# Two more conv channel tiles in the in-projection's second part

## The chip, the cores and the metric

One core of one Trainium2 chip runs the whole kernel, in one launch. The metric is the device time of an execution in microseconds (us); smaller is better. Engines are named as in the profile: PE (TensorE), DVE (VectorE), ACT (ScalarE), POOL (GpSimd) and SP (SyncE, which here only issues DMAs).

## The reference

One layer of a decoder trunk over 1024 positions of 1024 channels, all float32:

```
h = rms_norm(x, g_mix)
z = h @ w_in + b_in                      # 1024 -> 7168
va, ga, xb, gb, sa, sb = split(z, [1024, 1024, 1536, 1536, 1024, 1024])

u = va * sigmoid(ga)
u = causal_depthwise_conv(u, width 31)
y_a = silu(layer_norm(u)) @ w_a_out

v = causal_depthwise_conv(xb, width 4)
r = sigmoid(v @ w_a + b_a), i = sigmoid(v @ w_x + b_x)     # 16 heads of 96, block-diagonal
a = exp(-8 r softplus(-lam));  v = scan(h = a h + sqrt(1 - a^2) i v)
y_b = (v * gelu(gb)) @ w_b_out

x = x + (sigmoid(sa) * y_a + sigmoid(sb) * y_b) @ w_o
x = x + square(relu(rms_norm(x, g_mlp) @ w_1)) @ w_2
out = rms_norm(x, g_final)
```

## The kernel before

Channels lie on the 128 partitions, positions along the free axis. z has 56 tiles of 128 channels: 8 of va, 8 of ga, 12 of xb, 12 of gb, 8 of sa, 8 of sb. Each float32 operand of a product is split in a high and a low part, and a product is three matmul passes (high x high, low x high, high x low). Weights are split by `split_dma`: ACT writes the negative weight into the low tile (L65), a POOL DMA adds the weight to it (L66), ACT writes the high tile (L67).

**First part of the in-projection** (43 to 361 us). Tiles are computed one by one, in the order of the list `CH`. A tile is 48 matmuls (`chunk_mm`, L726): 8 blocks of input channels x 3 passes x 2 halves of the positions. The loop over s takes one tile of `CH` a turn; such a turn is called a slot here. Slot s also evacuates tile s-1 on ACT and DVE:

- an xb tile becomes v by the conv of width 4 (`xb_out`: xb L474, v L477 on ACT, the rest on DVE, L486), and `xb_parts` splits v (vth on ACT L494, vtl on DVE);
- a pair of va and ga becomes u = va x sigmoid(ga) (`u_out`, sigmoid L589 on ACT, the rest on DVE).

The 16 heads of the recurrence run in the same slots. Slot s of head n (`HS0[n]` = s): three quarters of the tile's matmuls, then the gate product of the head before (`head_mm(before, 1)`), the rest of the tile, then `head_mm(n, 0)`, the first gate product of the new head. Each is 6 matmuls (L534 to L536) on pieces of v (`head_load`, tiles vh and vl, loaded by SP at the end of the slot before). ACT reads the product with a sigmoid (`head_gate`, L542), and SP moves the gate to full tiles (L549). PSUM holds four tiles of 128 x 1024: three under the tag "ps" for the channel tiles, and one under "ps2" for all gate products (`PS`, L48). Heads stand in `HS0` in groups of four with one slot between (5-8, 10-13, 15-18, 20-23); a group's heads use three tiles of v. In the slot behind a group's last head (`EXP`: 9, 14, 19, 24) ACT computes the group's exponentials and tanh (`scan_exp`, L558, L559), in the next its square roots (`scan_root`, L566); then DVE runs the scans (`scan_tile`, L575 to L578, hd written by SP at L579). Exponentials, square roots and sigmoids each need their table loaded on ACT (ACT_TABLE_LOAD rows). The order of ACT's work in a slot is the order of these lines (shortened):

```
before, new, nxt = (head_at.get(s + d) for d in (-1, 0, 1))
if before is not None:
    head_gate(before, 0, begun)
    head_mm(before, 1)
...                                  # evacuation of tile s-1, weights of tile s+1
if s - 1 in EXP:
    scan_root(EXP[s - 1])
if s == 3 or c >= XB:
    vector_work(0)
    xb_parts(0 if s == 3 else c - XB)
if before is not None:
    head_gate(before, 1, clk["P"] - 12 * MM)
...                                  # then scan_exp in the slots of EXP
```

**Second part** (361 to 630 us). The other tiles are taken in pairs (`ZPAIRS`, 14 of them: gb, sa, sb), each as a 2 x 2 block product by Strassen's scheme with seven products of 12 matmuls (`z_mm`, L914) instead of eight. Its right sides are sums of quarters of the normalized input: `x_load` loads four xs tiles, `x_sum` forms the differences on DVE, `x_parts` splits them (xs6h, xs6l and so on); `XS` and `ZX` say in which slot. Its left sides are sums of quarters of the weights (`z_sums`, zs on DVE), split by `z_lhs` (zo). `z_out` evacuates a quarter: gb is multiplied with the scan's output, sa and sb are spilled as sigmoids.

**The conv of width 31** runs on DVE alone: for each of the eight u tiles some 48 operations (`conv`, taps L637), with a sum over tiles (ysum L651) for the layer norm's mean. A planner keeps a clock for PE, ACT and DVE (`clk`, `at`); `later` notes DVE work with a due time, `vector_work` issues it and fills what is left with taps. Order on each engine is fixed when the program is built.

**After it**: the product with w_b_out (8 tiles of 72 matmuls, `b_mm`, L1097), in which the conv's output is loaded again (`n_load`) and its mean formed (`n_mean`); then w_a_out, w_o and the MLP.

Of the kernel before, what the change touches and what calls it, by code (L numbers as in the profile page):

```python
# [15 lines left out]
P = 128  # L16
# [3 lines left out]
NH = 16  # L20
# [10 lines left out]
def trunk_kernel(ctx: ExitStack, tc: tile.TileContext, x, xt_in, xt_eo, vecs, w_in, w_a_out, w_b_out,  # L31
# [550 lines left out]
    yd = dp.tile([8, P, S], F32, name="yd")  # L582
    ysum = []

    def u_out(j, psv, psg):

        u = T(f"u{j}")
        uv = u.rearrange("p (o n) -> p o n", o=2)
        nc.scalar.activation(uv, psg.rearrange("p (n o) -> p o n", o=2), AF.Sigmoid,  # L589
                             bias=bin_c[:, GA + j:GA + j + 1])  # L590
        later(at("A", 1.11), 1.28, nc.vector.scalar_tensor_tensor, uv,
              psv.rearrange("p (n o) -> p o n", o=2), bin_c[:, VA + j:VA + j + 1], uv,
              ALU.add, ALU.mult)
        ut[j] = u
        fresh.append(j)


# [86 lines left out]
                later(at("A", 1.0), 1.2, nc.vector.tensor_tensor, l, src, h.bitcast(F32),  # L684
                      ALU.subtract)

    CH = [XB, VA, GA, XB + 1, XB + 2]
    for js, g in (((1,), 1), ((2,), 2), ((3,), 3), ((4, 5, 6, 7), 4)):
        CH += [c for j in js for c in (VA + j, GA + j)]
        CH += [XB + t for t in range(3 * g, min(3 * g + 3, 12))]  # L690
    NC1 = len(CH)
    zps = {n: z0[n] for n in range(N0)}
    wraw, wst = {}, {}
# [33 lines left out]
                                 start=n == 0, stop=n == 23)  # L727
        at("P", len(halves) * (n1 - n0) * MM)

    ZPAIRS = [GB + 2 * i for i in range(6)] + [SA + 2 * i for i in range(4)]  # L730
    ZPAIRS += [SB + 2 * i for i in range(4)]
    NZ = len(ZPAIRS)
    zraw, zs, zo, zb = {}, {}, {}, {}
# [2 lines left out]
    def z_load(i, kk):  # L736

        zraw[i, kk] = raw = qp.tile([P, 2, 4, P], F32, tag="p", name=f"zw{i}_{kk}", bufs=4)
        c = ZPAIRS[i]
        nc.sync.dma_start(raw, w_in[c:c + 2, :, 4 * kk:4 * kk + 4, :].rearrange("m p k c -> p m k c"))  # L740

    def z_blk(i, m_, kk):
# [45 lines left out]
    def z_get(n, f):  # L788
# [1 line left out]

    ENGINES = {mybir.EngineType.Activation, mybir.EngineType.DVE, mybir.EngineType.PE,
               mybir.EngineType.SP, mybir.EngineType.Pool}
    HS0 = [5 + 5 * (n // 4) + n % 4 for n in range(NH)]
    head_at = {s: n for n, s in enumerate(HS0)}

    EXP = {head_slot: g for g, head_slot in enumerate(HS0[4 * g + 3] + 1 for g in range(4))}
    XS = {23: ((x_load, 0),), 24: ((x_sum, 0),), 25: ((x_load, 1), (x_parts, 0, 6)),
          26: ((x_sum, 1), (x_parts, 0, 7, 5)), 27: ((x_parts, 0, 4), (x_parts, 1, 6))}
    w_load(3)
    w_load(4)  # L800
    for c2 in range(4):
# [2 lines left out]
    with tc.manual_schedule(engines=ENGINES):  # L804
        for s in range(3, NC1):
            w_load(s + 2)
            taps["hold"] = s > NC1 - 4
            begun = clk["P"]
            clk["A"], clk["V"] = max(clk["A"], begun + 0.5), max(clk["V"], begun - 2)

            if s == 3:

                chunk_mm(s, 0, 24, (1,))
                rs = first_scale()
                first_product(0, rs)
# [10 lines left out]
            if s > 3:  # L826
                chunk_mm(s, 18, 24)
            if new is not None:
                head_mm(new, 0)

            c = CH[s - 1]
            if c >= XB:
                xb_out(c - XB, zps[s - 1])
            elif c >= GA:
                u_out(c - GA, zps[s - 2], zps[s - 1])
            w_parts(s + 1)
            if s - 1 in EXP:

# [6 lines that stand above are left out]
            if nxt is not None:  # L845
                head_w_parts(nxt)
            if s == 5:
                decay_on()
            if s + 2 in head_at:
                head_w(head_at[s + 2])  # L850
            for d in range(5):
                if s - d in EXP:
                    g = EXP[s - d]
                    if d == 0:
                        scan_exp(g)
                        scan_in(begun + 3.5, 3 * g, 3 * g + 1)
# [49 lines left out]
    def z_mm(i, p):  # L906
# [9 lines left out]
                n += 1  # L916
        at("P", 12 * MM)

    def z_out(i, m_, hf, src, name):
        ci = ZPAIRS[i] + m_  # L920
        bias = bin_c[:, ci:ci + 1]
        if ci < SA:
# [19 lines left out]

    def z_h(i, m_, hf):
        t = ZPAIRS[i] + m_ - GB
        if t < 12:
            hb[t, hf] = h = EV(f"hb{t}_{hf}")
            nc.sync.dma_start(h, hd[t, :, HALVES[hf]])

# [26 lines left out]
        elif p == 4:  # L975
            z_out(i, 1, 0, zb[i, "u"], "c")

    ZX = {0: ((x_parts, 1, 7),), 7: ((later, 0, 4.8, scan_tile, 11),), 2: ((x_parts, 1, 5),), 4: ((x_parts, 1, 4),)}
    H_AT = {2: (0, 0), 5: (1, 1), 3: (0, 1), 4: (1, 0)}
    with tc.manual_schedule(engines=ENGINES):  # L980

# [36 lines left out]
        vector_work(clk["V"])  # L1018
        z_get(2, z_lhs)
        z_get(3, z_lhs)  # L1020
        u_out(7, zps[NC1 - 2], zps[NC1 - 1])
        vector_work(clk["V"])
        z_h(0, 0, 0)
        for n in range(len(zseq) + 2):
# [61 lines left out]
    def b_mm(j):  # L1086
# [11 lines left out]
        at("P", 72 * MM)  # L1098

    def b_out(j):  # L1100
        ps = bps.pop(j)
# [7 lines left out]

    q, mean, vacc, rstd = {}, {}, {}, {}  # L1110

    def n_load():
        for o in range(2):
            for kk in range(2):
                for c2 in range(2):
                    q[kk, o, c2] = a = T(f"q{kk}{o}{c2}")
                    for i in range(2):
                        nc.sync.dma_start(a[:, HALVES[i]], yd[4 * kk + 2 * c2 + i, :, HALVES[o]])

    def n_pieces(o):  # L1120
        return [(kk, c2, i) for kk in range(2) for c2 in range(2) for i in range(2)]
# [977 lines left out]
```

## Time and profile before

| | before |
|---|---|
| runs, us | 1545.78, 1543.67, 1544.39 (median 1544.39) |
| profiled execution, span, us | 1542.9 |
| PE busy | 1533.1 us (99%), 6782 instructions |
| DVE busy | 1222.5 us (79%) |
| ACT busy | 903.6 us (59%) |
| POOL busy | 184.4 us (12%) |
| granted TensorE clock, mean | 0.999 |
| first part, second part, product with w_b_out, us from the start | 43 to 361, 361 to 623, 623 to 760 |

The span runs from the first to the last instruction of one execution; the page gives no total of its own for that execution, and the median of the three runs stands 1.5 us above the span. A row of a timeline or of the chain has start, length (us), engine, line and operation, "out<-in" by the program's names, the count, and in brackets the engine's idle time ahead of it and what released it. Rows of stretches have start:end, length, then busy time and count for PE, PEld (weight load), DVE, ACT, POOL, and the granted clock, the share of the DMA engines and GB/s.

### The profile page before, as it was taken

The page shows a single profiled execution, that of the slowest core. Times are in us where ns is not written, and L with a number is a line of the kernel's source. Part 1 is how long each engine was busy: PE and PEld are TensorE (multiplying, and loading weights), DVE is VectorE, ACT ScalarE, POOL GpSimd, SP SyncE. Part 2 cuts the span into 40 slices and gives each one's busy share as a digit, 9 for nine tenths or more (in the row PEclk, how much of TensorE's full clock was granted, in tenths as well). Part 3 has the DMA queues.
Part 4 walks back from the last instruction along what each step waited for, and adds up shares of the span by engine and source line. Part 5 has one row for each costly group of instructions (what it writes and reads, how often), then busy time and mean ns, then how long its engine had stood idle before and what let it go on. Part 6 is the DMA issues. An engine that isn't in the chain of part 4 may idle for free.

```text
span 1542.9 us, 19178 instructions
## 1 busy us (share of the span) xinstructions
PE 1533.1 (99%) x6782; PEld 1262.4 (82%) x6782; DVE 1222.5 (79%) x1648; ACT 903.6 (59%) x1261; POOL 184.4 (12%) x219
## 2 busy tenths in 40 slices
PE   9999999999999999999999999999999999999998
PEld 8888788888888888888888887888888888888886
DVE  6899999979899997478569879755555558888897
ACT  6648576567567667345275777554444475555553
POOL 0000000002222222000022332000000001111110
PEclk9999999999999999999999999999999999999999
DMA  8776978898997879953579898333333779888862
GB/s 347 197 189 161 251 187 222 217 280 217 247 253 196 193 191 246 327 157 116 182 201 299 197 193 204 137 122 112 113 114 111 241 216 228 223 222 224 209 130 110
DMA packets 132288, 307.82 MB, mean 200 GB/s; under 512 B 13232, under 2 KB 35248, under 8 KB 132192
## 3 DMA queue, kind: packets, MB, share of 16 engines
q1 hardware_dynamic: 101744, 230.60, 46.0%
q0 software_dynamic: 30304, 75.74, 26.9%
q8 instruction: 53, 0.87, 0.2%
q14 instruction: 43, 0.35, 0.1%
q10 hardware_dynamic: 144, 0.26, 0.0%
HBM read 147.69 MB, written 58.72 MB: 134 GB/s over the span
## 4 chain that ended last, share of the span: by engine, by line
PE 95%; DMA 2%; issue 1%; DVE 1%; SPq 0%; POOL 0%; ACT 0%; POOLq 0%; DVEq 0%
PE z L726 18%; PE d L1863 15%; PE yb L1097 8%; PE e L1983 3%; PE keep L1863 2%; PE z L258 1%; PE rg L534 1%; PE rg L536 1%; PE rg L535 1%; DMA x<-in_x_dram 1%; DMA gu<-w_raw 1%; DMA xc<-in_xt_dram 0%; PE go3f L1274 0%; PE f15d L1550 0%; PE f15c L1550 0%
## 5 line engine op out<-in xcount | busy, mean ns | idle before, releaser
L726 PE MATMUL z<-xh,win_h 128*128 128x512 f32 x400 | 124.9, 390 | 0.0
L726 PE MATMUL z<-xl,win_h 128*128 128x512 f32 x400 | 124.5, 389 | 0.0
L1875 DVE TENSOR_TENSOR acc<-acc,d 128x1024 f32<-128x1024 f32 x72 | 87.8, 1219 | 33.3 <-PE d L1863 32.6
L726 PE MATMUL z<-xh,win_l 128*128 128x512 f32 x400 | 98.2, 391 | 0.0
L726 PEld LDWEIGHTS z<-xh,win_l 128*128 128x128 f32 x400 | 75.1, 188 | 16.9
L726 PEld LDWEIGHTS z<-xh,win_h 128*128 128x128 f32 x400 | 75.0, 188 | 16.7 <-ACT win_h L67 0.7
L637 DVE SCALAR_TENSOR_TENSOR y<-u,vec,y 128x511 f32<-128x511 f32 (+14 forms) x120 | 88.3, 736 | 0.0
L726 PEld LDWEIGHTS z<-xl,win_h 128*128 128x128 f32 x400 | 75.1, 188 | 15.8
L542 ACT ACTIVATE g<-rg,vec 96x1024 f32<-96x1024 f32 x32 | 35.6, 1113 | 85.5 <-issue 46.0
L637 DVE SCALAR_TENSOR_TENSOR y<-yt,csum,y 128x511 f32<-128x511 f32 (+6 forms) x112 | 82.5, 736 | 0.0
L637 DVE SCALAR_TENSOR_TENSOR yt<-u,vec,yt 128x511 f32<-128x511 f32 (+6 forms) x112 | 82.5, 736 | 0.0
L66 POOL DMA_DIRECT2D win_l<-win_raw x25 | 21.8, 871 | 324.3 <-ACT win_l L65 312.3
L1538 ACT ACTIVATE o<-s 128x512 fp32r<-128x512 f32 x56 | 33.7, 623 | 45.7 <-DVE s L1522 26.4
L66 POOL DMA_DIRECT2D zo<-zw x42 | 36.6, 871 | 129.4 <-ACT zo L65 116.1
L1097 PE MATMUL yb<-hgl,wb_h 128*128 128x512 f32 x168 | 51.7, 389 | 0.0
L1097 PE MATMUL yb<-hgh,wb_h 128*128 128x512 f32 x168 | 51.7, 389 | 0.0
L486 DVE SCALAR_TENSOR_TENSOR v<-xb,vec,v 128x1023 f32<-128x1023 f32 (+2 forms) x36 | 46.2, 1282 | 6.9 <-ACT v L477 6.1
L66 POOL DMA_DIRECT2D db_1l<-wr x7 | 6.1, 870 | 310.5 <-ACT db_1l L65 287.9
L1097 PE MATMUL yb<-hgh,wb_l 128*128 128x512 f32 x168 | 41.0, 389 | 0.0
L65 ACT ACTIVATE zo<-zw 128x512 fp32r<-128x512 f32 x42 | 26.3, 625 | 20.7 <-PE z10f L914 2.1
L1063 DVE TENSOR_TENSOR o<-s,o 128x512 fp32r<-128x512 f32 x56 | 37.3, 683 | 0.5 <-ACT o L1538 0.5
L1097 PEld LDWEIGHTS yb<-hgh,wb_h 128*128 128x128 f32 x168 | 31.5, 188 | 6.6
(1805 smaller groups left out, 4669.7 us busy)
## 6 DMA issues: line engine op xcount, KB each, us to landing
w_raw<-in_w_dram SPq DMA_DIRECT2D x34, 512.0 KB, 5.7
fr<-fd SPq DMA_DIRECT2D x32, 512.0 KB, 6.3
wr<-in_w_dram SPq DMA_DIRECT2D x32, 512.0 KB, 6.6
zw<-in_w_in_dram SPq DMA_DIRECT2D x28, 512.0 KB, 6.3
win_raw<-in_w_in_dram SPq DMA_DIRECT2D x25, 512.0 KB, 6.8
win_l<-win_raw POOLq DMA_DIRECT2D x25, 512.0 KB, 6.7
zo<-zw POOLq DMA_DIRECT2D x42, 256.0 KB, 5.6
gates<-zg SPq DMA_DIRECT2D x32, 256.0 KB, 3.9
```

Of the source, the lines that this page charges most:

```text
L65: nc.scalar.activation(l, src, AF.Copy, scale=-1.0)
L66: nc.gpsimd.dma_start(l, src, accum_op=ALU.add)
L486: nc.vector.scalar_tensor_tensor(v[:, d:S], a[:, 0:S - d], cbw_c[:, w * 12 + t:w * 12 + t + 1], v[:, d:S], ALU.mult, ALU.add)
L542: nc.scalar.activation(a, gps.pop((n, gi))[:HD, :], AF.Sigmoid, bias=(ba_c, bx_c)[gi][:, n:n + 1])
L637: nc.vector.scalar_tensor_tensor(o[:, k:], a[:, 0:HS - k], c, o[:, k:], ALU.mult, add)
L726: nc.tensor.matmul(zps[s][:, HALVES[hf]], w[:, k, :], xw[k][part][hf], start=n == 0, stop=n == 23)
L1063: tt(l, src, h.bitcast(F32), ALU.subtract)
L1097: nc.tensor.matmul(ps[hf], a, b[:, HALVES[hf]], start=n == 0, stop=n == len(todo) - 1)
L1538: nc.scalar.activation(o[:, 0], src, AF.Copy)
L1863: nc.tensor.matmul(o, a, b, start=n == 0 and (p != 1 or g == 0), stop=n == len(todo) - 1, skip_group_check=p == 1 and g > 0)
L1875: tt(acc[p, q2], acc[p, q2], ps, ALU.add)
L1983: nc.tensor.matmul(o, a, b, start=n == 0 and t not in LOADED, stop=n == len(todo) - 1, skip_group_check=t in LOADED)
```

## The change

- `NU = 6`: `CH` has va and ga of six conv tiles instead of eight, 24 tiles at its end instead of 28 (the first three are computed ahead of the loop). Its order becomes XB, VA, GA, XB1, XB2, GA1, XB3, VA1, XB4, XB5, GA2, XB6 to XB8, VA2, XB9 to XB11, then GA and VA of 3, 4, 5. ga now comes ahead of va, so `u_out` is cut in `u_gate` (the sigmoid) and `u_out` (the product), each with its own tile.
- `HS0` becomes 4 to 8 and 10 to 20: one slot without a new head (9) instead of three between the groups. `EXP` follows: 8, 13, 17, 21. Head 8 starts in 13, head 12 in 17.
- `ZPAIRS` gets the pairs (VA+6, GA+6) and (VA+7, GA+7) at places 6 and 8, 16 pairs in all. Their weights are loaded by two DMAs for each half; `z_out` hands them to the new `z_u`, which forms u6 and u7 by halves.
- `x_load`, `x_sum` and `x_parts` move to the last four slots; three of the x parts, (0,4), (1,6) and (1,7), go to the second part's first and second product.
- Of all groups the scans follow their roots by the same offset; `n_load` goes from j = 0 to j = 1 of the product with w_b_out, `n_mean` into the middle of tile 2.

```diff
-    CH = [XB, VA, GA, XB + 1, XB + 2]
-    for js, g in (((1,), 1), ((2,), 2), ((3,), 3), ((4, 5, 6, 7), 4)):
-        CH += [c for j in js for c in (VA + j, GA + j)]
-        CH += [XB + t for t in range(3 * g, min(3 * g + 3, 12))]
+    NU = 6
+    CH = [XB, VA, GA, XB + 1, XB + 2, GA + 1, XB + 3, VA + 1, XB + 4, XB + 5, GA + 2]
+    CH += [XB + 6, XB + 7, XB + 8, VA + 2, XB + 9, XB + 10, XB + 11]
+    CH += [c for j in range(3, NU) for c in (GA + j, VA + j)]
...
-    ZPAIRS = [GB + 2 * i for i in range(6)] + [SA + 2 * i for i in range(4)]
+    ZPAIRS = [GB + 2 * i for i in range(6)] + [VA + 6, SA, VA + 7] + [SA + 2 * i for i in range(1, 4)]
     ZPAIRS += [SB + 2 * i for i in range(4)]
...
+        if c < GA:
+            for m_, col in enumerate((GA + c, VA + c)):
+                nc.sync.dma_start(raw[:, m_], w_in[col, :, 4 * kk:4 * kk + 4, :])
+            return
...
-    HS0 = [5 + 5 * (n // 4) + n % 4 for n in range(NH)]
+    HS0 = [4 + n + int(n > 4) for n in range(NH)]
...
-    XS = {23: ((x_load, 0),), 24: ((x_sum, 0),), 25: ((x_load, 1), (x_parts, 0, 6)),
-          26: ((x_sum, 1), (x_parts, 0, 7, 5)), 27: ((x_parts, 0, 4), (x_parts, 1, 6))}
+    XS = {NC1 - 4: ((x_load, 0),), NC1 - 3: ((x_sum, 0),), NC1 - 2: ((x_load, 1), (x_parts, 0, 6)),
+          NC1 - 1: ((x_sum, 1), (x_parts, 0, 7, 5))}
+    head_w(0)
...
-                u_out(c - GA, zps[s - 2], zps[s - 1])
+                u_gate(c - GA, zps[s - 1])
+                if c == GA:
+                    u_out(0, zps[1])
+            elif s > 3:
+                u_out(c - VA, zps[s - 1])
...
-                    t = 3 * g + d - (2 if g < 3 else 1)
+                    t = 3 * g + d - 1
...
+    def z_u(i, j, m_, hf, src):
+
+        if m_ and hf:
+            return
+        if (m_, hf) == (0, 0):
+            uz[j] = T(f"u{j}")
+        d = halved(uz[j], hf)
+        if m_ == 0:
+            nc.scalar.activation(d, src.rearrange("p (n o) -> p o n", o=2), AF.Sigmoid,
+                                 bias=bin_c[:, GA + j:GA + j + 1])
+            ready = at("A", 0.62)
+            if hf == 0:
+                return
+            src = zb[i, "c"]
...
-    ZX = {0: ((x_parts, 1, 7),), 7: ((later, 0, 4.8, scan_tile, 11),), 2: ((x_parts, 1, 5),), 4: ((x_parts, 1, 4),)}
+    ZX = {0: ((x_parts, 0, 4), (x_parts, 1, 6)), 1: ((x_parts, 1, 7),), 2: ((x_parts, 1, 5),),
+          4: ((x_parts, 1, 4),), 7: ((later, 0, 4.8, scan_tile, 11),)}
...
+            if j == 2 and n == 18:
+                n_mean()
...
-                n_load()
-            if j == 2:
-                n_mean()
...
             if j < 2:
+                if j:
+                    n_load(*range(7))
                 vector_work(math.inf if j else clk["P"] - 0.3)
+                if j:
+                    n_load(7)
```

More of the change, by code (lines that the diff above doesn't have):

```diff
@@ L583, in trunk_kernel, with u_gate, u_out @@
     ysum = []
[L585 to L592, printed above, removed]
+    def u_gate(j, ps):
+        ut[j] = u = T(f"u{j}")
+        nc.scalar.activation(u.rearrange("p (o n) -> p o n", o=2), ps.rearrange("p (n o) -> p o n", o=2),
+                             AF.Sigmoid, bias=bin_c[:, GA + j:GA + j + 1])
+        at("A", 1.11)
+    def u_out(j, ps):
+        uv = ut[j].rearrange("p (o n) -> p o n", o=2)
+        later(clk["A"], 1.28, nc.vector.scalar_tensor_tensor, uv,
+              ps.rearrange("p (n o) -> p o n", o=2), bin_c[:, VA + j:VA + j + 1], uv,
               ALU.add, ALU.mult)
-        ut[j] = u
         fresh.append(j)
@@ L917, in z_mm @@
         at("P", 12 * MM)
+    uz = {}
+    def z_u(i, j, m_, hf, src):
[11 more added lines that the diff above has]
+            src = zb[i, "c"]
+        else:
+            ready = 0
+        later(ready, 0.74, nc.vector.scalar_tensor_tensor, d,
+              src.rearrange("p (n o) -> p o n", o=2), bin_c[:, VA + j:VA + j + 1], d,
+              ALU.add, ALU.mult)
+        if hf:
+            ut[j] = uz.pop(j)
+            fresh.append(j)
     def z_out(i, m_, hf, src, name):
+        if ZPAIRS[i] < GA:
+            z_u(i, ZPAIRS[i] - VA, m_, hf, src)
+            return
         ci = ZPAIRS[i] + m_
@@ L944, in z_h @@
         t = ZPAIRS[i] + m_ - GB
-        if t < 12:
+        if 0 <= t < 12:
             hb[t, hf] = h = EV(f"hb{t}_{hf}")
@@ L1020, in trunk_kernel @@
         z_get(3, z_lhs)
-        u_out(7, zps[NC1 - 2], zps[NC1 - 1])
+        u_out(NU - 1, zps[NC1 - 1])
         vector_work(clk["V"])
@@ L1095, in b_mm @@
         for n, (a, b) in enumerate(todo):
+            if j == 2 and n == 18:
+                n_mean()
             for hf in range(2):
                 nc.tensor.matmul(ps[hf], a, b[:, HALVES[hf]], start=n == 0, stop=n == len(todo) - 1)
-        at("P", 72 * MM)
+            at("P", 2 * MM)
     def b_out(j):
@@ L1110, in trunk_kernel, with n_load @@
     q, mean, vacc, rstd = {}, {}, {}, {}
-    def n_load():
+    def n_load(*js):
         for o in range(2):
[L1114 to L1118, printed above, removed]
+            for j in js:
+                k = j // 4, o, j % 4 // 2
+                if k not in q:
+                    q[k] = T(f"q{k[0]}{o}{k[2]}")
+                nc.sync.dma_start(q[k][:, HALVES[j % 2]], yd[j, :, HALVES[o]])
     def n_pieces(o):
```

## The prediction

> **What bounds the kernel now.** I read the stretches first, then the chain of waits, then the engine timelines round each place where the change moves something. The rows of the stretches give start and end, length, and each engine's busy time with its count; then the granted TensorE clock.
>
> ```profile
> span 1542.9 us, 19178 instructions
> ...
> 43.00:361.00 318.00, 317.99 (x1393) 256.16 (x1392) 295.74 (x379) 204.86 (x216) 26.14 (x30) 1.00 0.83 217
> 361.00:623.00 262.00, 262.00 (x1157) 216.94 (x1157) 234.73 (x349) 174.03 (x293) 57.55 (x66) 1.00 0.86 220
> 623.00:760.00 137.00, 137.00 (x606) 113.40 (x605) 83.92 (x109) 54.34 (x75) 0.00 (x0) 1.00 0.57 186
> ```
>
> The reader is to see that PE never stands still: 317.99 of 318 us in the first part of the in-projection, 262.00 of 262 in the second, 137.00 of 137 in the stage after it. Two things follow. A matmul taken away is worth its full time, and any new wait of PE is paid in full, since nothing else hides it. DVE, second busiest, works 295.74 of 318 us (93%) in the first part and 90% in the second; ACT has room on average (204.86 of 318), so what counts there is the order of its work, not the amount.
>
> **PE's own work.** The chain of waits in the first part is PE alone (start, length, what):
>
> ```profile
> 42.91 10.88 PE z L726 x48
> ...
> 128.03 13.65 PE z L726 x60
> ...
> 151.35 0.23 PE rg L534
> ...
> 152.75 2.77 PE z L726 x12
> ...
> 156.90 8.18 PE z L726 x36
> ...
> 166.48 2.77 PE z L726 x12
> 169.25 0.24 PE rg L534
> ...
> 360.98 2.72 PE z0a L914 x12
> ...
> 383.42 2.72 PE z1b L914 x12
> ```
>
> A channel tile of the first part is 48 matmuls in 10.88 us; a product of the second part is 12 matmuls in 2.72 us. Four tiles leave the first part (4 x 10.88 = 43.5 us) and two pairs of seven products join the second (14 x 2.72 = 38.1 us). Net -24 matmuls: **-5.4 us**, and this is the only gain that PE's count can give.
>
> **Where the heads now meet the exponentials.** The heads' gate products (rg, L534 to L536) all go through one PSUM tile, so the next head's first gate cannot start until ACT has read this head's second gate (g, L542). In the kernel before, slots without a new head lie between the groups of four, and the exponentials (L558, L559) and square roots (L566) of the scan fall there. In the changed order head 8 starts in the slot of the second group's exponentials (13), and slot 14 holds its square roots, head 8's second gate and head 9's first; slots 17 and 18 do the same for heads 12 and 13. ACT's timeline of before shows that work for the first group, with no idle time between its rows (start, length, line, operation):
>
> ```profile
> 129.19 1.10 ACT L542 ACTIVATE g<-rg,vec 96x1024 f32<-96x1024 f32 x1
> 130.19 0.35 ACT L522 ACTIVATE rgh<-rraw 96x192 fp32r<-96x192 f32 x1
> 130.56 1.28 ACT L558 ACT_TABLE_LOAD   x1
> ...
> 138.56 1.09 ACT L474 ACTIVATE xb<-z,vec 128x1024 f32<-128x1024 f32 x1
> ...
> 142.84 1.28 ACT L566 ACT_TABLE_LOAD   x1
> 144.14 2.96 ACT L566 ACTIVATE g<-g 128x1024 f32<-128x1024 f32 x3
> 147.00 1.05 ACT L494 ACTIVATE vth<-v 128x1024 fp32r<-128x1024 f32 x1
> ...
> 148.32 1.28 ACT L542 ACT_TABLE_LOAD   x1
> 149.61 1.12 ACT L542 ACTIVATE g<-rg,vec 96x1024 f32<-96x1024 f32 x1
> ...
> 152.78 1.11 ACT L542 ACTIVATE g<-rg,vec 96x1024 f32<-96x1024 f32 x1 [0.16 <-PE rg L536]
> ```
>
> From one head's second gate (129.19) to the end of the next gate behind the roots (149.61 + 1.12 = 150.73) ACT needs 21.54 us. In slots 13 and 14 the built program has the same list, with one gate more in it (head 8's first, which comes between exponentials and roots and needs a table load of its own: 1.28 + about 1.02) and one rgh less (0.37): 21.54 + 2.3 - 0.4 = 23.5 us until head 8's second gate is read. PE, from the end of head 7's second gate product, has a remainder of a tile, a gate product, three quarters of a tile, a gate product and a remainder: in before this is 152.75 to 169.25, 16.5 us. Then head 9 must wait: 23.5 - 16.5 = 7.0 us. ACT picks the first gate up 0.16 us (row at 152.78) to 1.16 us (129.19 against PE's end at 128.03) after PE; with 0.4 us for this, **7.4 us a time, 14.8 us for two** (between 13 and 16.4). In before ACT had finished at 150.73 what PE wanted at 151.35 in this same place; the margin was 0.6 us.
>
> **Slots 8 to 10.** Group one has the free slot (9), but head 4 now starts in slot 8 and its first gate stands behind the exponentials. In before the list from 129.19 to the last of them ends at 138.56, and the new gate with its table load ends 2.4 us later, 141.0; PE wants the bank at 128.03 + 2.77 + 1.39 + 8.18 = 140.4 (a gate product takes 1.39: 155.52 to 156.90). That is **0.6 us** (0 to 1.2). Head 5's operands are pieces of tile 4, whose vth now comes behind slot 9's roots, and their loads stand on SP's queue behind the write of scan 0, which runs on DVE at the same time:
>
> ```profile
> 149.21 1.22 DVE L462 TENSOR_TENSOR vtl<-v,vth 128x1024 fp32r<-128x1024 f32 x1
> ...
> 150.61 1.21 DVE L575 SCALAR_TENSOR_TENSOR g<-a,g 128x1024 f32<-128x1024 f32 x1
> ...
> 153.25 2.29 DVE L578 TENSOR_TENSOR_SCAN g<-a,g 128x1024 f32<-128x1024 f32 x1
> ...
> 157.19 0.50 SPq L511 DMA_DIRECT2D vh<-vth  x1
> ...
> vl<-vtl SPq DMA_DIRECT2D x8, 256.0 KB, 5.5
> ```
>
> Counted from the start of the root slot (130.80 in before, which is 128.03 + 2.77), roots end at 147.10 - 130.80 = 16.3 there, and at 16.3 + 2.3 (the extra gate) - 1.4 (one gate product more on PE ahead of the slot) = 17.2 in the changed order; vth follows, 18.2. The scan takes 4.9 us (150.61 to 155.54) and can start after the first root, the low part takes 1.2: done between 21.3 and 23.3, I take 22.3. Issue 1.7 us later (155.54 to the load at 157.19), landing 5.5 us after it: 29.5. PE wants it at two tiles and a gate product, 10.88 + 1.39 + 10.88 = 23.2, plus 0.5 to the first use of a low part and the 0.6 above: 24.3. **5.2 us** (2 to 8).
>
> **The start of the second part.** Its right sides are sums of four quarters (xs), loaded late in the first part. Before: loads in slot 23, five before the end. After: in the fourth slot from the end, so every later step of this list stands one slot, 10.9 us, nearer to the second part.
>
> ```profile
> 320.67 1.23 DVE L462 TENSOR_TENSOR xs<-xs,xs 128x1024 f32<-128x1024 f32 x1 [7.42 <-DMA xs<-xu]
> ...
> 371.10 0.69 DVE L462 TENSOR_TENSOR zs<-zs,zw 128x512 f32<-128x512 f32 x1
> ...
> 374.20 0.87 POOL L66 DMA_DIRECT2D zo<-zs  x1 [10.38 <-ACT zo L65]
> ...
> zo<-zs POOLq DMA_DIRECT2D x7, 256.0 KB, 6.6
> ```
>
> DVE's first sum waits for the loads (7.42 us of idle time), 40.3 us ahead of the second part's first matmul (360.98 - 320.67); that becomes 29.4. The list behind it is DVE's and hardly shorter: the conv taps were already held back in these slots. The operand that suffers most is the weight sum of pair 1 for z1b: made at 371.10, its low part issued at 374.20 and landed 6.6 us later, 380.8, for a matmul at 383.42, a margin of 2.6 us. With 10.9 us less it is 8.3 us late. Earlier operands (low parts of the third and fourth products, the sixth x sum) are late by less, and what PE waits there counts towards the 8.3. I take **7 us** in all (2 if DVE catches up by leaving idle time out, 12 if the two x parts that moved behind the border also queue in front).
>
> **What costs nothing.** DVE gets four sums, two low parts and two additions more for each moved pair, all of half a tile (0.69 us, row at 371.10), some 11 us for both, in a second part that grows by 38.1 us and in which it had 27 us idle; if that cover is gone it costs what DVE lacks, at most 11. The pair's weights come by two 256-KB loads instead of one of 512, the second of them six products (16 us) ahead. Sums of the first mean and the reload of the conv outputs go to later places of the next stage, where DVE works 83.92 of 137 us. None waits before PE does; if the last conv came late it would cost a part of one of its eight tiles of 17 us (137 / 8).
>
> **The clock.** PE has no gap in the middle of before. The only long one is its end:
>
> ```profile
> 1535.77 0.61 PE L1983 MATMUL e<-lb22l,la22h 128*128 128x512 f32 x2
> ...
> 1537.00:1540.00 3.00, 0.00 (x0) 0.00 (x0) 1.61 (x6) 1.13 (x4) 0.00 (x0) 1.00 0.02 8
> 1540.00:1543.00 3.00, 0.00 (x0) 0.00 (x0) 0.00 (x0) 0.00 (x0) 0.00 (x0) 0.57 0.45 167
> ```
>
> The last matmul ends at 1536.4; the clock is 1.00 up to 1540, then 0.57 on the mean of three us, which a fall to one half at 1540.4 would give: 4.0 us without a matmul. A wait of 7.4 us passes that, one of 5 only just. How long the clock stays low is shown nowhere here. If as long as it takes to fall, PE loses half of 4.0 us each time: 2.0, for the two long waits **4.0 us** (0 if it recovers at once, 6 if slot 10's counts too). [...]
>
> **The sum.** -5.4 + 14.8 + 0.6 + 5.2 + 7.0 + 4.0 = +26.2 us. On the profiled span, 1542.9 + 26.2 = 1569.1; the median of the runs, 1544.39, is 1.5 above the span, so **1570.6**. The low ends of the same terms give -5.4 + 13 + 0 + 2 + 2 + 0 = +11.6, 1556; the high ends -5.4 + 16.4 + 1.2 + 8 + 12 + 6 = +38.2, 1583.
>
> **Rivals.** *Only ACT's lists bite* (0.15): the x parts and head 5's pieces arrive, because DVE has fewer taps ahead of them than I think. For it: waits on ACT put work of DVE, SP and POOL ahead at no cost. Against it: both chains begin in a DMA landing (7.42 us of DVE idle time), not in a lack of DVE. -5.4 + 14.8 + 4.0 = +13.4: 1558, and 1554 without the clock's share. *More is late* (0.11): DVE, with 93% already, is not done with its sums when the second part asks, the margin of the following pairs is gone as well, and the full high ends apply: 1580 to 1590. *Faster* (0.08): the single bank's hand-over is covered. The place is the second gate of heads 8 and 12; the point from which it decides is an ACT list of 16.5 us instead of 23.5, which would need the exponentials (about 8 us with their load) to run ahead of head 7's second gate, and head 5 and the x sums to keep their margins. Then only the matmuls count: -5.4, 1539. Against it: all rows from 129.19 to 150.73 are back to back, and the order on ACT is fixed. *No difference* (0.02): gain and a single wait cancel, 1541 to 1547. That the change doesn't take effect is out: its four tiles are gone from the built program.
>
> **How the numbers follow.** The forecast, all three kinds of wait, has 0.64. The range 1553 to 1583 takes in its bounds and the first rival, 0.79, and a little of the second. A measurement of this kernel tells about 0.2%, 3.1 us, from no change; faster by more than that 0.08, within it 0.02, slower 0.90.
>
> **What would show it.** In the profile after: two idle times of PE near 7 us ahead of an rg of L534, released by ACT's g of L542; one near 5 released by the vh or vl load; several short ones ahead of z0b, z1b and their neighbours, 7 in sum; the clock below 1.00 just behind the long ones; and a second part that begins near 342, not at 317.5 (360.98 less 43.5). If PE has no idle time ahead of rg there, the reading of ACT's list is wrong, and with it most of the forecast. If the second part starts without waits, the tail is the wrong step.

## The result: 36.8 us slower

The changed kernel takes 1581.15 us (median; 1580.54 to 1581.74), the one before 1544.39: a ratio of 1.0238, 95% interval 1.0226 to 1.0251. Forecast were 1570.6 us and a range of 1553 to 1583. The sign, the range and the kinds of wait hold; the sum was 10.6 us too small, and two of its terms, head 5's pieces and the clock, account for nearly all of that (4.2 and 6.4 us).

The stretches of the changed kernel, cut at the first matmul of each part (columns as before):

```profile
core 0 of [0], span 1579.6 us
42.91:351.06 308.15, 282.84 (x1201) 224.23 (x1200) 245.22 (x313) 193.74 (x202) 19.41 (x23) 0.95 0.77 200
351.06:659.22 308.16, 302.22 (x1326) 249.45 (x1324) 283.08 (x416) 199.56 (x337) 69.84 (x80) 0.99 0.83 210
659.22:797.09 137.87, 137.87 (x610) 114.12 (x609) 96.70 (x128) 55.02 (x75) 0.00 (x0) 1.00 0.57 191
```

PE, which stood still nowhere in these parts before, is now idle for 25.3 us in the first and 6 us in the second, and the granted clock, 1.00 before, is 0.95 and 0.99. The first part should have shrunk by 43.5 us and shrank by 9.9 (318.07 to 308.15); the second should have grown by 38.1 and grew by 46.1. The stage after it is the same on PE (137.87 us in both), though DVE does 11.9 us more in it (84.79 before), 9.5 of them late conv taps, at no cost.

All PE waits over 0.7 us between 43 and 600 us, from its timeline (in brackets the idle time and what ended it):

```profile
131.27 0.47 PE L534 MATMUL rg<-vh,rgh 96*96 96x512 f32 x1 [0.77 <-ACT g L542]
151.89 0.71 PE L534 MATMUL rg<-vh,rgh 96*96 96x512 f32 x1 [5.27 <-DMA vh<-vth]
157.11 0.71 PE L536 MATMUL rg<-vl,rgh 96*96 96x512 f32 x1 [4.09 <-DMA vl<-vtl]
220.92 0.74 PE L534 MATMUL rg<-vh,rgh 96*96 96x512 f32 x1 [7.29 <-ACT g L542]
285.69 0.74 PE L534 MATMUL rg<-vh,rgh 96*96 96x512 f32 x1 [7.31 <-ACT g L542]
360.21 0.50 PE L926 MATMUL z0a<-xh,zo 128*128 128x512 f32 x1 [3.10 <-ACT z0b L992]
366.09 0.80 PE L926 MATMUL z1a<-xh,zo 128*128 128x512 f32 x1 [2.85 <-ACT z1b L992]
```

These are the places that the sum named: slot 9's gate, head 5's pieces, the gates of heads 9 and 13, the start of the second part. One of 0.57 us (head 3's first gate, slot 7) was not in it. The full account of the profiled execution (1542.9 to 1579.6, +36.7):

| term | forecast | measured |
|---|---|---|
| matmuls | -5.4 | -5.4 |
| second gate behind the roots, slots 14 and 18 | 14.8 | 14.6 |
| other gates | 0.6 | 1.3 |
| head 5's pieces | 5.2 | 9.4 |
| start of the second part | 7.0 | 6.0 |
| what is left: slower matmuls behind the waits | 4.0 | 10.4 |
| elsewhere | 0 | 0.4 |

The measured 10.4 is worked out: first part 308.15 - (318.07 - 43.52) - 25.3 = 8.3, second part 308.16 - (262.03 + 38.08) - 5.95 = 2.1.

**The list on ACT.** The same list as in before, with the gate (207.95) that the prediction put into it:

```profile
197.16 1.12 ACT L542 ACTIVATE g<-rg,vec 96x1024 f32<-96x1024 f32 x1 [0.37 <-PE rg L536]
...
206.66 1.28 ACT L542 ACT_TABLE_LOAD   x1
207.95 1.11 ACT L542 ACTIVATE g<-rg,vec 96x1024 f32<-96x1024 f32 x1
...
213.25 1.28 ACT L566 ACT_TABLE_LOAD   x1
214.54 2.95 ACT L566 ACTIVATE g<-g 128x1024 f32<-128x1024 f32 x3
217.40 1.04 ACT L494 ACTIVATE vth<-v 128x1024 fp32r<-128x1024 f32 x1
218.46 1.28 ACT L542 ACT_TABLE_LOAD   x1
219.75 1.11 ACT L542 ACTIVATE g<-rg,vec 96x1024 f32<-96x1024 f32 x1
```

From 197.16 to 219.75 + 1.11 = 220.86 it takes 23.7 us (forecast 23.5), and PE's next gate product starts at 220.92.

**The clock.** Rows of one us in and behind that wait; PE's last matmul before it ended at 213.6 (the clock is the third column from the right):

```profile
214.00:215.00 1.00, 0.00 (x0) 0.00 (x0) 0.98 (x1) 0.99 (x2) 0.00 (x0) 1.00 1.08 209
215.00:216.00 1.00, 0.00 (x0) 0.00 (x0) 1.00 (x2) 1.00 (x2) 0.00 (x0) 0.84 1.11 209
...
225.00:226.00 1.00, 1.00 (x4) 0.81 (x3) 0.97 (x2) 1.00 (x2) 0.00 (x0) 0.54 1.11 303
226.00:227.00 1.00, 1.00 (x6) 0.79 (x6) 1.00 (x1) 0.83 (x1) 0.82 (x1) 1.00 1.01 205
```

The rows between them show 0.50. So a mean of 0.84 means one half from 215.7 on, 2.1 us after the last matmul; 0.54 means full clock again from 225.9, 5.0 us after PE began to work at 220.92. At the low clock gate matmuls start every 0.43 us (222.31, 222.74), at full clock every 0.23 (120.78, 121.01). So PE loses 2.5 us there, half of the 5.0. Read in the same way, the wait in slot 18 costs 2.5 us, the two for head 5 together 2.5, and the second wait at the start of the second part 1.6: 9.1 of the 10.4.

### The profile page after: what moved, and what is told of

It reads as the page before. It is cut to its first block, busy times and chain, and to the rows that moved or that the text cites. A ratio compares the mean times of both kernels' runs of the same rounds, so it can differ in the third digit from the quotient of the medians.

```text
span 1579.6 us, 19214 instructions
## 1 busy us (share of the span) xinstructions
PE 1538.3 (97%) x6758; PEld 1262.7 (80%) x6758; DVE 1232.4 (78%) x1666; ACT 918.4 (58%) x1290; POOL 190.4 (12%) x225
## 4 chain that ended last, share of the span: by engine, by line
PE 84%; DVE 5%; ACT 4%; issue 4%; DMA 2%; POOL 1%; SPq 0%; POOLq 0%; DVEq 0%; ACTq 0%
PE d L1907 14%; PE yb L1140 8%; PE z L729 7%; PE e L2027 3%; PE keep L1907 2%; PE z L258 2%; DVE y L640 1%; ACT g L542 1%; PE rg L534 1%; ACT a L558 1%; DVE yt L640 1%; PE rg L536 1%; DMA vl<-vtl 1%; DVE v L486 1%; PE rg L535 1%
## 5 line engine op out<-in xcount | busy, mean ns | idle before, releaser
L729 PE MATMUL z<-xh,win_h 128*128 128x512 f32 x336 | 107.4, 397 | 0.0
L729 PE MATMUL z<-xl,win_h 128*128 128x512 f32 x336 | 106.2, 394 | 0.0
L729 PE MATMUL z<-xh,win_l 128*128 128x512 f32 x336 | 83.0, 391 | 0.0
L729 PEld LDWEIGHTS z<-xh,win_h 128*128 128x128 f32 x336 | 64.7, 193 | 15.0 <-ACT win_h L67 0.7
L729 PEld LDWEIGHTS z<-xl,win_h 128*128 128x128 f32 x336 | 64.2, 191 | 13.9
L729 PEld LDWEIGHTS z<-xh,win_l 128*128 128x128 f32 x336 | 63.1, 188 | 14.4
L66 POOL DMA_DIRECT2D zo<-zw x48 | 42.0, 874 | 157.1 <-ACT zo L65 142.4
L66 POOL DMA_DIRECT2D win_l<-win_raw x21 | 18.3, 873 | 317.5 <-ACT win_l L65 274.7
L534 PE MATMUL rg<-vh,rgh 96*96 96x512 f32 x64 | 27.1, 424 | 21.2 <-ACT g L542 15.9
L65 ACT ACTIVATE zo<-zw 128x512 fp32r<-128x512 f32 x48 | 30.0, 625 | 23.6 <-issue 4.2
```

The costliest lines, as they stand in the source:

```text
L66: nc.gpsimd.dma_start(l, src, accum_op=ALU.add)
L534: nc.tensor.matmul(o, gh[:, gi, :], vh[:, hs], start=True, stop=False)
L729: nc.tensor.matmul(zps[s][:, HALVES[hf]], w[:, k, :], xw[k][part][hf], start=n == 0, stop=n == 23)
```

## The experiments

Each run is compared with the kernel before on the same chip. Differences between two runs are differences of their medians, in part from different chips, on which the kernel before differs by up to 0.9 us (1543.61 to 1544.52). Theory and rival are those of the quoted texts.

**The second gate ahead of the roots** (gate_first).

```diff
             if s - 1 in EXP:
+                if before is not None:
+                    head_gate(before, 1, clk["P"] - 12 * MM)
                 scan_root(EXP[s - 1])
...
-            if before is not None:
+            if before is not None and s - 1 not in EXP:
                 head_gate(before, 1, clk["P"] - 12 * MM)
```

> Edit: in the slots of the square roots (9, 14, 18) ACT reads the second gate of the head before (L542) ahead of the roots, not behind them; all else as in the changed kernel. Theory (ACT's list between two second gates holds PE in slots 14 and 18): the list from head 7's second gate to head 8's loses two table loads, three roots and a vth (6.4 us), so each wait falls from 7.3 to between 1 and 2 us, and the time that PE then spends at half clock (some 2.5 us a time) goes with it: 1581 - 2 x 5.8 - 2 x 2.5 = about 1565. Head 5's wait for its vh and vl pieces (9.4 us) stays within 2 us, since vth is still behind the roots. Rival (the slots are limited by DVE or by DMA, and ACT is only the last to say so): the waits move to vh, vl or the next tile's weights, and the time stays within 4 us of 1581.

1572.83 us, ratio 1.0189 (1.0174 to 1.0204). PE's timeline:

```profile
152.66 0.71 PE L534 MATMUL rg<-vh,rgh 96*96 96x512 f32 x1 [6.10 <-DMA vh<-vth]
211.78 0.47 PE L534 MATMUL rg<-vh,rgh 96*96 96x512 f32 x1 [0.67 <-ACT g L542]
229.44 0.71 PE L534 MATMUL rg<-vh,rgh 96*96 96x512 f32 x1 [3.71 <-DMA vh<-vth]
292.70 0.71 PE L534 MATMUL rg<-vh,rgh 96*96 96x512 f32 x1 [4.58 <-issue]
```

Both waits of 7.3 us are down to 0.67 and 0.81, so the cause is the place in ACT's order. But the time fell by 8, not by 16: 3.7 and 4.6 us come back one slot later, at the first gate product of heads 10 and 14. On SP their pieces stand behind a scan's write, as head 5's do (hd at 220.10, the first vh at 220.48). The long wait on ACT had covered this second one. Nor did the clock's share go: the rows of the clock show four stretches at one half here too, and the mean granted clock is 0.989, as in the changed kernel. Head 5's wait, expected to stay at 9.4, fell to 6.1. Both theory and rival were half right.

**The scans one slot later** (scan_later).

```diff
-                    t = 3 * g + d - 1
+                    t = 3 * g + d - (2 if g < 3 else 1)
```

> Edit: the scans of the first three groups one slot later, as in the kernel before; all else as in the changed kernel. Theory (head 5's pieces are late because scan 0 stands ahead of vtl on DVE and its hd write ahead of them on SP): vtl about 3 to 4 us earlier, and the loads no longer behind a 512-KB write; the two waits of 5.27 and 4.09 us come to 4 to 5 together: about 1576. Waits of 7.3 us in slots 14 and 18 unchanged. Rival (the loads are slow because the DMA engines are full in this place, whatever stands ahead of them): the landing stays near 9 us and the time within 2 us of 1581.

1576.96 us, ratio 1.0213 (1.0198 to 1.0228).

```profile
149.41 0.44 PE L534 MATMUL rg<-vh,rgh 96*96 96x512 f32 x1 [2.79 <-DMA vh<-vth]
150.55 0.71 PE L536 MATMUL rg<-vl,rgh 96*96 96x512 f32 x1 [0.47 <-DMA vl<-vtl]
```

Head 5's wait falls from 9.4 to 3.3 us; the time falls by 4.2 us, within 1 us of the theory. What made the wait 9.4 and not 5.2 in the changed kernel stands in the rows of SP and in the chain (kernel after):

```profile
144.31 0.72 SPq L579 DMA_DIRECT2D hd<-g  x1
145.12 0.54 SPq L511 DMA_DIRECT2D vh<-vth  x1
...
147.39 0.57 SPq L511 DMA_DIRECT2D vl<-vtl  x1
```

```profile
147.39 9.59 DMA vl<-vtl
```

The last vl piece was issued at 147.39. The slot began at 122.2 (head 4's gate product, 120.78, and its 1.39 us), so that is 25.2 us into the prediction's count, which had 22.3 + 1.7 = 24.0. But it landed 9.6 us later instead of 5.5. The scan's 512 KB of hd, issued just ahead, and 512 KB of weights, issued just behind (148.05), were on their way too. So the step's order was right, and the landing time, taken from a median of the kernel before, was not. In scan_later, where the scan's write no longer stands ahead, the last piece is issued only 1.0 us earlier and lands in 4.0 us, though the weights are still issued just behind it:

```profile
146.39 4.03 DMA vl<-vtl
```

```profile
147.03 0.64 SPq L60 DMA_DIRECT2D win_raw<-in_w_in_dram  x1
```

So of the 6.6 us by which the piece comes earlier, 5.6 are its landing and 1.0 its issue, and it is the scan one slot later that does it. The rival, a landing that stays near 9 us, is out.

**PE kept busy in the two waits** (clock_busy).

```diff
+            if new in (9, 13):
+                zps[s + 1] = PS(f"z{s + 1}")
+                for _ in range(28):
+                    nc.tensor.matmul(zps[s + 1][:, HALVES[0]], wst[s][0][:, 0, :], xw[0][0][0],
+                                     start=True, stop=True)
             if new is not None:
                 head_mm(new, 0)
```

> Edit: 28 matmuls that nothing reads (6.3 us) into the next tile's PSUM just ahead of the first gate of heads 9 and 13, where PE waits 7.3 us; all else as in the changed kernel. Theory (a wait of that length drops the granted clock to one half, and PE pays some 2.5 us after each): the clock stays at 1.00 behind both places and the time falls by 4 to 5 us, to about 1576.5, though work was added. Rival (the slow matmuls behind the waits have another cause, or PE catches up): the time stays within 1 us of 1581.

1577.06 us, ratio 1.0208 (1.0191 to 1.0225); the changed kernel's was 1.0238. PE waits 0.94 and 0.98 us at the two places, with 6.3 us of matmuls that nothing reads in front, and the time is 4.1 us lower. The granted clock now stays at 1.00 behind both places, where the changed kernel lost 2.5 us each; its mean over the execution is 0.994 (changed kernel 0.989). Work added in a wait gained time: the clock's term is real. The 4.1 is not a clean measure of it, since head 5's waits, which lie ahead of the edit, came out 1.2 us shorter in this execution (8.1) and the clock there stayed low for longer (148.7 to 162.3).

**The x parts behind ACT's copies** (x_behind).

```diff
-    ZX = {0: ((x_parts, 0, 4), (x_parts, 1, 6)), 1: ((x_parts, 1, 7),), 2: ((x_parts, 1, 5),),
+    ZX = {1: ((x_parts, 1, 6),), 2: ((x_parts, 1, 7),), 3: ((x_parts, 0, 4), (x_parts, 1, 5)),
```

> Edit: the x parts that were moved behind the border are issued one or two products later, behind ACT's copies z0b and z1b (L992): (1,6) at product 1, (1,7) at 2, (0,4) with (1,5) at 3. All else as in the changed kernel. Theory (the waits of 3.10 and 2.85 us at z0a and z1a come from ACT's copies standing behind these parts): both waits go below 0.5 and the lower clock behind them too: 1581 - 6 - 2 = about 1573. Rival (the x sums themselves are late on DVE, as the prediction had it for z1b): the waits move to z0b, z0f or z1b and at most 2 us are won.

1579.96 us, ratio 1.0232 (1.0217 to 1.0248). The two waits fall from 5.95 to 1.65 us, and a new one appears at z0b:

```profile
370.00 0.53 PE L926 MATMUL z0b<-xs6l,zo 128*128 128x512 f32 x1 [2.25 <-DVE xs6l L462]
```

The rival holds in its numbers: 1.2 us are won, and the wait moves to z0b. What is late there is the low part xs6l; it stands on DVE behind the x sums, weight sums and a scan. Which product waits is a matter of order on ACT and DVE.

**Gate, vth, then roots, and the scans later** (order_all).

```diff
             if s - 1 in EXP:
+                if before is not None:
+                    head_gate(before, 1, clk["P"] - 12 * MM)
+                if c >= XB:
+                    vector_work(0)
+                    xb_parts(c - XB)
                 scan_root(EXP[s - 1])
-            if s == 3 or c >= XB:
+            elif s == 3 or c >= XB:
...
-            if before is not None:
+            if before is not None and s - 1 not in EXP:
...
-                    t = 3 * g + d - 1
+                    t = 3 * g + d - (2 if g < 3 else 1)
```

> Edit: in the slots of the square roots ACT reads the second gate first, then makes vth, then the roots; and the scans of groups one to three one slot later, as in before. All else as in the changed kernel. Theory (the second gate's place on ACT holds PE in slots 14 and 18, and once that is gone the next heads wait for pieces whose vth stands behind the roots and whose load stands behind a scan's hd write): all of the waits on gates and pieces in slots 9 to 19 together fall from 25 us to under 6, and the half clock behind them goes: part one near 281 us instead of 308, the time near 1553. What is left is the start of the second part (6 us and its clock). Rival (the pieces are late because the DMA engines are full there): vh and vl waits of 3 to 6 us stay in three slots, and the time is 1562 or more.

1566.39 us, ratio 1.0142 (1.0127 to 1.0157), 15 us below the changed kernel and 13 above the theory. The waits in slots 9 to 19 fall to 11.4 us, not under 6. Two of them are long, 4.1 us on vh, whose pieces again stand behind a scan's write (hd issued at 154.44; the vh issued at 156.15 landed 8.4 us later), and this one on the gate in the slot after the roots; ACT's row gives its cause:

```profile
224.26 0.74 PE L534 MATMUL rg<-vh,rgh 96*96 96x512 f32 x1 [5.03 <-ACT g L542]
```

```profile
216.20 1.06 ACT L494 ACTIVATE vth<-v 128x1024 fp32r<-128x1024 f32 x1 [6.83 <-DMA vh<-vth]
```

vth can't be written before an earlier vh load has read its memory; ACT stands still for 6.8 us with the roots and the next gate behind it. Neither theory nor rival had that; the start of the second part still waits 4.5 us.

**One pair instead of two** (n7x). `NU = 7`, heads in 4-7, 9-12 and 14-21, the x steps one slot earlier, the order of order_all:

```diff
+    HS0 = [4 + n + int(n > 3) + int(n > 7) for n in range(NH)]
+    ZPAIRS = [GB + 2 * i for i in range(6)] + [VA + 7, SA] + [SA + 2 * i for i in range(1, 4)]
```

> Edit: as order_all, but only one pair (va7, ga7) moves to the second part: 26 tiles in the first, heads in 4-7, 9-12 and 14-21, x steps one slot earlier. PE has 12 matmuls less than before (-2.7 us). Theory: with two free slots and the x steps at their place of before, waits come to 1 to 3 us: 1541 to 1545, no difference from before that can be measured. Rival (a moved pair costs by itself, in the second part): 1547 or more, with waits in the pair's products.

1566.19 us, ratio 1.0143 (1.0128 to 1.0158). The theory is wrong by 21 us, but not for the rival's reason: PE waits up to 6.07 us for vh in the first part and 4.9 us at the second part's first products, none in the pair's own. One pair costs as much as two here; the waits lie in the order of the first part and at the border. With the x steps where they stood in before, the border waits all the same, now on DVE (z0a, 3.96 us, released by u, L462).

**Heads without a free slot, the x steps one slot earlier** (dense_so).

```diff
-    HS0 = [4 + n + int(n > 4) for n in range(NH)]
+    HS0 = [4 + n for n in range(NH)]
...
-    XS = {NC1 - 4: ((x_load, 0),), NC1 - 3: ((x_sum, 0),), NC1 - 2: ((x_load, 1), (x_parts, 0, 6)),
-          NC1 - 1: ((x_sum, 1), (x_parts, 0, 7, 5))}
+    XS = {NC1 - 5: ((x_load, 0),), NC1 - 4: ((x_sum, 0),), NC1 - 3: ((x_load, 1), (x_parts, 0, 6)),
+          NC1 - 2: ((x_sum, 1), (x_parts, 0, 7, 5)), NC1 - 1: ((x_parts, 0, 4), (x_parts, 1, 6))}
```

> Edit: as order_all, and heads in slots 4 to 19 without any free slot (xb tiles one slot earlier, va1 and va2 later), so that the last exponentials and roots come one slot earlier, and the x loads, sums and parts stand one slot earlier too, where they stood in before relative to the second part. Theory (the start of the second part waits because the x steps are one slot nearer to it than in before): its waits of 6 us go below 2, at the price of one more gate behind exponentials (0.7 us): near 1546. Rival (DVE as a whole is behind by the end of the first part): the waits at z0a to z1b stay at 4 us or more, or come back at later products; 1551 or more.

1556.62 us, ratio 1.0076 (1.0059 to 1.0093), 10 us above the theory: the wait at the border is 4.5 us and not below 2. No wait on pieces is left, though all heads are packed. Two rows of PE near the border, and the reason for the second on ACT:

```profile
314.02 3.94 PE L729 MATMUL z<-xh,win_l 128*128 128x512 f32 x16 [2.94 <-DMA win_l<-win_raw]
334.13 1.22 PE L931 MATMUL z0a<-xh,zo 128*128 128x512 f32 x2 [4.48 <-DMA zo<-zw]
```

```profile
325.41 1.28 ACT L588 ACT_TABLE_LOAD   x1 [4.53 <-DMA xs5l<-xs]
```

ACT's next instruction writes u5, into memory that the DMA of xs5l is still reading; the split of the second part's weights (zo) stands behind it. So the time is the rival's, but not by its cause alone: this wait is for memory.

**Three x parts one step later** (dense_t, against dense_so).

```diff
-    XS = {NC1 - 5: ((x_load, 0),), NC1 - 4: ((x_sum, 0),), NC1 - 3: ((x_load, 1), (x_parts, 0, 6)),
-          NC1 - 2: ((x_sum, 1), (x_parts, 0, 7, 5)), NC1 - 1: ((x_parts, 0, 4), (x_parts, 1, 6))}
+    XS = {NC1 - 5: ((x_load, 0),), NC1 - 4: ((x_sum, 0),), NC1 - 3: ((x_load, 1),),
+          NC1 - 2: ((x_parts, 0, 6), (x_sum, 1), (x_parts, 0, 7)), NC1 - 1: ((x_parts, 0, 5), (x_parts, 1, 6))}
```

> Edit against dense_so: the x parts (0,6), (0,5) and (0,4) one step later each ((0,6) behind the next slot's weights, (0,5) in the last slot, (0,4) at the second part's third product). Theory (in dense_so ACT stands still for 4.5 us ahead of u5, since u5's tile is the memory that the POOL DMA of xs5l still reads, and for 4.6 us ahead of xs6h, since that waits for a scan's tile; both push the weights behind them): the waits at win_l (2.9 us) and at the second part's zo (4.5 us and some 3 of half clock) go: 1556.6 - 10 = about 1547. Rival (the late weights come from the loads or from ACT's amount of work there): the waits stay within 2 us of these sizes, 1554 or more.

1550.99 us, ratio 1.0046 (1.0029 to 1.0063), 4 us above the theory. The wait at zo is down to 0.54 us, as the theory has it; that at win_l is still 2.1. The stretches:

```profile
42.87:326.96 284.09, 276.51 (x1201) 219.46 (x1200) 237.60 (x293) 197.20 (x207) 20.22 (x24) 1.00 0.84 221
326.96:627.90 300.94, 300.40 (x1325) 248.42 (x1324) 278.51 (x417) 196.98 (x334) 69.00 (x79) 1.00 0.85 212
```

The second part, with both pairs in it, takes 300.94 us where its matmuls need 262.03 + 38.08 = 300.1: the pairs themselves cost little but their matmuls. The clock is back at 1.00. In the first part 9.5 us are still lost (284.09 - 274.55), 4.4 in six short waits on gates and 3.2 in two on weights. The last 2.0 lie in PE's busy time, at full clock. In a run, gate matmuls start every 0.23 us though each lasts 0.40 (changed kernel, rows at 120.78 and 121.01), so a break should cost some 0.2 us more than its idle time, 1.9 for the eight: an estimate that no run tries.

**ACT's order in each slot** (tuned and dense_u, against dense_t). Both bring the weights ahead of xb in the slots of the roots and ahead of the sigmoid in slots without an xb tile, and in the slots of the roots the second gate ahead of v. In the other slots tuned puts the second gate ahead of vth everywhere, dense_u only in the slots of the exponentials. The roots stand behind vth in tuned, as in dense_t, and ahead of it in dense_u. The last of these, dense_u against tuned (the other lines are left out):

```diff
+            if root:
+                scan_root(EXP[s - 1])
             if s == 3 or c >= XB:
                 vector_work(0)
                 xb_parts(0 if s == 3 else c - XB)
-            if root:
-                scan_root(EXP[s - 1])
```

> Edit against dense_t: in every slot the second gate ahead of vth; in the slots of roots it comes right behind xb, and the weights ahead of both; in slots without an xb tile the weights ahead of the sigmoid. Theory (the six short waits on gates, 4.3 us together, and that for win_h, 1.8 us, are places in ACT's order): they go to under 2 us in all, 4 to 5 us below dense_t: near 1542.5, where PE's matmuls alone would give 1539. Rival (what ACT does earlier it then lacks for vth, and heads wait for pieces): no gain, vh waits of some us instead.

1568.82 us, ratio 1.0159 (1.0143 to 1.0176): worse by 18 us. No head waits for pieces, so the rival's cause is out as well. The gates of the next slot are late, up to 4.2 us. The roots stand behind vth, as in dense_t, but v now comes behind the weights and the gate, so DVE starts on it later and ACT stands still for 4.0 us ahead of vth, where it was 1.2:

```profile
139.31 1.06 ACT L497 ACTIVATE vth<-v 128x1024 fp32r<-128x1024 f32 x1 [4.04 <-issue]
```

> Edit against dense_t: in the slots of the roots ACT's order is first gate, weights, xb, second gate, v, roots, vth (the roots now fill the time in which vth waits for DVE); in the slots of the exponentials the second gate comes ahead of vth; in slots without an xb tile the weights come ahead of the sigmoid; all other slots as in dense_t. Theory (the six waits on gates and the one on win_h that are left in dense_t, 5.5 us, are places in ACT's order): 2.5 to 4 us below dense_t: near 1547.5, still above before, since some 5 us of waits in the first part remain against 5.4 us of saved matmuls, and the wait at win_l. Rival (each us that ACT gives to the gates it takes from vth or from the weights): within 1 us of 1551, or above it, with vh or win waits in the place of those on gates.

1549.29 us, ratio 1.0031 (1.0019 to 1.0043). Waits on gates are down to 2.8 us and those on weights gone, but 1.8 us on vl and 2.4 at z0a take their place: 1.7 us won where 2.5 to 4 were expected, or 2.6 if each is set against the kernel before on its own chip. The intervals of the two ratios overlap, so that dense_u is faster than dense_t is not shown. It has the lowest time found with two pairs moved, 32 us below the changed kernel and still 4.8 above the one before.

## Why the prediction was right, and where it was off

- *What bounds the kernel.* Right. PE had no idle time before, and its new waits (31.3 us) and slower matmuls (10.4), less the 5.4 saved, are all but 0.4 of the 36.7. But a shorter wait is not a gain of the same size, since the clock's share moves too. In the profiled executions gate_first has 9.8 us less of waits and is 7.1 shorter, scan_later 6.3 and 3.7, dense_t against dense_so 5.4 and 9.2.
- *PE's own work.* -5.4 us, as dense_t's second part shows.
- *Second gate behind the roots.* Right to 0.2 us: 7.3 twice, list 23.7 us. It was read off one timeline of before, by adding what the new order puts in.
- *Slot 9.* 0.77 against 0.6. The wait of 0.57 us at head 3 was not seen.
- *Head 5's pieces.* The mechanism was right, the term mis-sized: 9.4 against 5.2, above its high end of 8. Issue came 1.2 us later than expected, the landing took 9.6 us instead of 5.5, and in scan_later, without the scan's write ahead, 4.0.
- *Start of the second part.* 6.0 against 7.0, but by another operand first: the prediction named the weight sum of z1b; PE waited for ACT's copies z0b and z1b, which stood behind the x parts:

```profile
358.64 1.04 ACT L686 ACTIVATE xs6h<-xs 128x1024 fp32r<-128x1024 f32 x1
359.59 0.57 ACT L992 ACTIVATE z0b<-z0a 128x512 f32<-128x512 f32 x1
...
364.50 1.06 ACT L686 ACTIVATE xs7h<-xs 128x1024 fp32r<-128x1024 f32 x1 [3.79 <-DVE g L578]
365.46 0.58 ACT L992 ACTIVATE z1b<-z1a 128x512 f32<-128x512 f32 x1
```

  The row at 364.50 shows more: xs7h had its sum by 358.5 (DVE's row 357.31, 1.22 us long), and ACT waited 3.79 us until a scan on DVE (L578) was done. The root that the prediction named, the x steps one slot nearer to the border, is shown only in part. With the steps moved back, n7x and dense_so have no wait for these copies there, but 3.96 and 4.48 us for other things (u on DVE, weights behind ACT's stop). Only dense_t, where three x parts also come later, waits less than 0.6, and dense_u, with the same x steps, waits 2.4 for z0b again.
- *The clock.* The largest error: 10.4 against 4.0, above its high end of 6. Two things were off. The fall comes 2.1 to 4.2 us after the last matmul, not at 4.0, so that head 5's waits and one of 2.85 us trigger it too: four places instead of two. And the recovery takes up to 5.1 us of work, where 4.0 were assumed. clock_busy takes the clock's share away at two of the four. 1.3 of the 10.4 us are not in the stretches at half clock; they may be of the kind estimated under dense_t.
- *The sum and its range.* 1581.15 lies in 1553 to 1583, but only 2 us below the upper end. Two terms passed their own high ends (9.4 against 8, 10.4 against 6); the range held because the second part's term, with a high end of 12, came to 6.0. That is luck in part. The second part began at 351.06, where 342 was named, and the same two terms make up the difference.
- *Rivals.* "Only ACT's lists bite" is out, head 5 and the border both waited. "More is late" named 1580 to 1590, so the time alone does not tell it from the forecast. The trace does: two sizes were larger, but the border waited less than forecast, and no pair after the first two waited.

## What to carry to other kernels

When a change removes the free slots between groups of work, follow one in-order engine through a slot and add up its list between two hand-overs of a single buffer: that sum against the bound engine's work between them gave the wait to 0.2 us, with nothing but rows of the kernel before. A wait on the bound engine hides the next one behind it, so taking the largest away gives back less than its size (13.1 us removed at two gates, 8 won), and moving an instruction earlier on an engine helps only if its own inputs and its memory are free by then (ACT stood still for 4.0 us ahead of vth in tuned, for 6.8 in order_all). On PE, a wait can come with a lower clock in it and behind it: in the changed kernel waits of 2.85 to 7.31 us had four stretches at 0.50, which cost 1.6 to 2.5 us of matmul time each, while one wait of 3.10 us cost nothing of the kind.

## What the runs showed of the hardware

In the changed kernel the granted clock fell from 1.00 to 0.50 at 150.8, 215.7, 280.5 and 365.9 and rose to 1.00 at 161.1, 225.9, 290.8 and 369.3 us. The fourth stretch, in rows of one us:

```profile
365.00:366.00 1.00, 0.00 (x0) 0.00 (x0) 1.00 (x2) 1.00 (x2) 0.00 (x0) 0.93 0.99 246
...
369.00:370.00 1.00, 1.00 (x6) 0.78 (x5) 1.00 (x3) 1.00 (x1) 0.00 (x0) 0.86 0.00 0
```

The first three stretches last 10.2 us and the fourth 3.4. The falls came 4.2 us after PE's last matmul in slot 10, 2.1 in slot 14, 2.2 in slot 18 and 2.6 at the start of the second part, and there was none in the wait of 3.10 us that ended at 360.21. So a wait's length alone did not tell whether the clock fell: with 2.85 us it did, with 3.10 it did not. What decides it is not shown. Within the four stretches PE worked 5.1, 5.0, 5.1 and 3.2 us before the clock was full again. In scan_later the clock fell at 150.3, after PE had gone back to work at 149.41.
